# Differential attention scores: the low queries' pass over latent keys as two 64-row matmuls

## The chip, the cores and the metric

The kernel runs on one core of a Trainium2 chip. The metric is the time of one execution in device microseconds; the time before is 2394.58 us, the median of three runs.

## The reference, cut to what matters

Two layers of a hybrid backbone over 512 latent tokens and 256 context tokens, D = 1024, f32. In each layer one of three token mixers is differential attention with 4 heads. A head has two maps, each with its own 64 channels of query and key; both share a value of 128 channels. Latent queries read latent and context keys in one softmax, context queries (first layer only) read context keys alone.

```
def diff_attend(q, k, v, lam):
    s = jnp.einsum('bqhmd,bkhmd->bhmqk', q, k, preferred_element_type=jnp.float32) * (ATTN_HD ** -0.5)
    p = jax.nn.softmax(s, axis=-1)
    a = p[:, :, 0] - lam * p[:, :, 1]
    return jnp.einsum('bhqk,bkhe->bqhe', a.astype(v.dtype), v)
```

Around it stand the input projection of every branch, a pooling branch, a long convolution, the gates, the output projection and a SwiGLU network, all with f32 inputs.

## The kernel before, in words

**Number format.** TensorE multiplies fp32r operands. To keep f32 accuracy each operand is split into a high part, rounded to fp32r, and a low part, the rest. A product is then made of high by high, high by low and low by high; low by low is left out.

**Scores.** A head's map has 64 channels, half the 128 partitions, so one key tile of 128 partitions holds both parts of one map. `roped` (lines 992 to 1016) writes them: for map m, `k[m]` has the high keys in "own" partitions (0 to 63 for map 0, 64 to 127 for map 1) and the low keys in the other 64. For the queries there are two tiles for a map: `qz[m][0]` has the high queries in both halves, so that one matmul of 128 partitions gives high by high plus high by low; `qz[m][1]` has the low queries in the own half and zeros in the other (set once by GpSimd, line 1190 and after), so that a second matmul adds low by high. The `qz` tiles are the stationary operand (128 queries), the keys the moving one.

**One call.** `weights(h, q0, lat)` (line 1042) makes the attention weights of 128 queries. For latent queries it takes three PSUM tiles: `sl[0]` and `sl[1]` (512 latent keys, one for each map; "s" in the rows, line 1053) and `sct` (256 context keys of both maps; "sc", line 1054). It issues eight matmuls, four of 512 columns and four of 256. Then VectorE takes the maxima, first of `sct` and then of each `sl` (lines 1056 and 1059), ScalarE the exponentials (1066, 1070), and both the normalised difference `aw`. For context queries (layer 0 only) there is `sct` alone.

**Order.** Each head makes four calls for latent queries (blocks 0 to 3) and in layer 0 two for context queries, then turns and multiplies by values, in the order of `HEAD`. Between those steps `fill()` sets units of the input projection: line 285, the kernel's most frequent matmul, three passes for a weight tile. The program's text does not fix the order in which an engine gets its instructions: a planner orders them when the program is built. On each engine it takes the earliest instruction in program order that by its own reckoning can start; one whose PSUM tile has not been released, or whose input isn't there, is passed by later ones. PSUM tiles of tag "x" are four in layer 0 and five in layer 1, and the transposes, values and statistics use them too.

**Other half-array matmuls.** `mlp_steps` (line 608) multiplies f32 tiles by 64 x 64 weights, for two directions in opposite corners of the array; in layer 1's filters this stands amid line 285's stream. `first_norm` (line 403) uses 32 columns of the array for each of four products.

Of the kernel before, what the change touches and what calls it, by code (L numbers as in the profile page):

```python
# [18 lines left out]
L = 512  # L19
C = 256  # L20
T = L + C
# [123 lines left out]
def build(ctx: ExitStack, tc: tile.TileContext, io: dict, out: bass.AP, dbg=None):  # L145
    nc = tc.nc
    V, A, PE, SP, G = nc.vector, nc.scalar, nc.tensor, nc.sync, nc.gpsimd
# [34 lines left out]
    def PT(tag, n, shape, dt=F32):  # L182
        pool, size, cnt = tg[tag]
        assert int(np.prod(shape[1:])) * 4 <= size, (tag, n, shape)
        return pool.tile(shape, dt, tag=tag, name=nm(n), bufs=cnt)
# [10 lines left out]
    def TB(n, dt=F32, shape=None):  # L196
        return PT("b", n, shape or [P, 512], dt)
# [5 lines left out]
    def SM(n, w, bufs=4):  # L203
        return sm.tile([P, w], F32, tag=f"sm{w}x{bufs}", name=nm(n), bufs=bufs)
# [13 lines left out]
    def PX(n="x"):  # L218
        return ps["pool"].tile([P, 512], F32, tag="x", name=nm(n), bufs=4 + ps["layer"])
# [689 lines left out]
    def layer(l, a, hs, first, prepare):  # L909
# [83 lines left out]
        qkv = [{} for _ in range(HEADS)]  # L993
# [48 lines left out]
        def weights(h, q0, lat):  # L1042

            qs = slice(q0, q0 + P)
            sl = [PX("s"), PX("s")] if lat else None
            sct = PX("sc")
            scs = [sct[:, m * 256:m * 256 + 256] for m in range(2)]
            for m in range(2):
                y = qkv[h]["k"][m]
                for pi, x in enumerate(qz[m]):  # L1050
                    kw = dict(start=(pi == 0), stop=(pi == 1))
                    if lat:
                        PE.matmul(sl[m][:], x[:, qs], y[:, 0:L], **kw)  # L1053
                    PE.matmul(scs[m], x[:, qs], y[:, L:T], **kw)  # L1054
            mx = SM("mx", 8, bufs=6)
            V.tensor_reduce(out=mx[:, 0:2], in_=sct[:].rearrange("p (m k) -> p m k", m=2), axis=AX.X, op=ALU.max)
            if lat:
                for m in range(2):
                    V.tensor_reduce(out=mx[:, 2 + m:3 + m], in_=sl[m][:], axis=AX.X, op=ALU.max)
                V.tensor_tensor(out=mx[:, 0:2], in0=mx[:, 0:2], in1=mx[:, 2:4], op=ALU.max)  # L1060
            V.tensor_scalar(out=mx[:, 4:6], in0=mx[:, 0:2], scalar1=-0.125, scalar2=None, op0=ALU.mult)
            su = SM("su", 8, bufs=6)
            ec = TB("ec")
            el = []
            for m in range(2):
                A.activation(ec[:, m * 256:m * 256 + 256], scs[m], AF.Exp, scale=0.125, bias=mx[:, 4 + m:5 + m],
                             accum_out=su[:, m:m + 1])
                if lat:
                    e = TB("el")
                    A.activation(e[:], sl[m][:], AF.Exp, scale=0.125, bias=mx[:, 4 + m:5 + m],  # L1070
                                 accum_out=su[:, 2 + m:3 + m])
                    el.append(e)
            if lat:
                V.tensor_tensor(out=su[:, 0:2], in0=su[:, 0:2], in1=su[:, 2:4], op=ALU.add)
            V.reciprocal(su[:, 4:6], su[:, 0:2])
            V.tensor_tensor(out=su[:, 6:7], in0=su[:, 5:6], in1=nlam[:, l:l + 1], op=ALU.mult)
            aw = PT("aw", "aw", [P, T])
            for e0, e1, c0, nn in (([(el[0][:], el[1][:], 0, L)] if lat else [])
                                   + [(ec[:, 0:256], ec[:, 256:512], L, C)]):
                A.activation(aw[:, c0:c0 + nn], e0, AF.Copy, scale=su[:, 4:5])  # L1080
                V.scalar_tensor_tensor(out=aw[:, c0:c0 + nn], in0=e1, scalar=su[:, 6:7],
                                       in1=aw[:, c0:c0 + nn], op0=ALU.mult, op1=ALU.add)
            return aw
# [105 lines left out]
        qz = [[PT("qz", "qz", [P, W], F32R) for _ in range(2)] for _ in range(2)]  # L1189
# [30 lines left out]
        for h in range(HEADS):  # L1220
# [4 lines left out]
            m = {}  # L1225
            aws = {}
            awc = None
            for what in HEAD[l]:
                if what == "f":
                    fill()  # L1230
                elif what == "r":
                    rest()
                elif what in "0123":
                    aws[int(what)] = weights(h, int(what) * P, True)
                elif what == "c":
                    awc = [weights(h, L + i * P, False) for i in range(2)] if cx else None
                elif what in "AB":
                    i = 0 if what == "A" else 2
                    m[what] = turn([aws[i], aws[i + 1]], True)
                else:  # L1240
                    values(h, m["A" if what == "V" else "B"], 0 if what == "V" else 256, ot)
# [284 lines left out]
```

## Time and profile before

| What | Value |
| --- | --- |
| Time, median of 3 runs (lowest to highest) | 2394.58 us (2389.93 to 2403.16) |
| The profiled execution's own time | 2393.87 us |
| Its span, first to last instruction | 2392.1 us |
| Mean granted TensorE clock | 0.991 |
| TensorE matmul records, share of the span | 2325.6 us, 97% |
| VectorE, ScalarE | 1722.3 us (72%), 983.6 us (41%) |

Instructions are named by line, engine, operation and tiles: "out<-in", without buffer numbers. For a matmul the shape is given as partitions x columns of the weights, then partitions x columns of the moving operand. PE is TensorE's matmul, PEld its weight load, which runs beside. The ends of matmuls are modelled: matmuls are pipelined, and a recorded end lies after the start of the next one, so the stream is read from starts. In a timeline, neighbours of one kind are merged into one entry, with their count and the time from the first start to the last end.

### The profile page before, as it was taken

Reading aid. Unit: us, or ns where it says so; the run is one execution under the profiler, and the core shown is the slowest. Engines: PE = TensorE matmul, PEld = TensorE weight load, DVE = VectorE, ACT = ScalarE, POOL = GpSimd, SP = SyncE. Lnnn points to the kernel's source line nnn. Section 1 sums busy time; section 2 is a strip of 40 time slices with the busy share of each in tenths; the row PEclk is TensorE's granted clock in tenths of the full one; section 3 lists DMA queues with packets and bytes.
Section 4 is the critical chain, followed back from the end, with each engine's and each line's share of the span. In section 5 each row is a group of like instructions: output and inputs, shape, how many; then the busy total and the mean of one; then the engine's idle time right before and its main releaser. Section 6 shows DMA issues by size and latency. Waiting matters only on the chain. (4 is left out here: it accounts for less than half of the span.)

```text
span 2392.1 us, 33306 instructions
## 1 busy us (share of the span) xinstructions
PE 2325.6 (97%) x12834; PEld 1981.7 (83%) x12834; DVE 1722.3 (72%) x3135; ACT 983.6 (41%) x1657; POOL 2.7 (0%) x8
## 2 busy tenths in 40 slices
PE   6999899999999999999999999999999999999998
PEld 3888688888878878888888888888888789888888
DVE  5688877999888785666768726899888778333336
ACT  6433334367762352121133424433377635312223
POOL 0000000000000000000000000000000000000000
PEclk9999899999989999999999999999999999999999
DMA  7222132321137543444725525344311444332324
GB/s 265 71 96 81 44 103 71 124 95 67 45 133 253 185 156 130 130 146 158 232 88 170 167 98 162 125 165 162 119 56 46 168 152 154 113 97 95 96 92 150
DMA packets 117801, 302.47 MB, mean 126 GB/s; under 512 B 13445, under 2 KB 27397, under 8 KB 116618
## 3 DMA queue, kind: packets, MB, share of 16 engines
q1 hardware_dynamic: 117642, 300.34, 37.9%
q8 instruction: 101, 1.65, 0.3%
q14 instruction: 58, 0.48, 0.1%
HBM read 266.74 MB, written 33.55 MB: 126 GB/s over the span
## 5 line engine op out<-in xcount | busy, mean ns | idle before, releaser
L252 ACT CAST wh<-wr 128x1024 fp32r<-128x1024 f32 (+3 forms) x327 | 331.0, 1013 | 933.2 <-PE d L285 756.1
L285 PE MATMUL d<-ah,wh 128*128 128x512 f32 (+1 forms) x2320 | 707.4, 354 | 6.8 <-ACT si L1371 2.8
L285 PE MATMUL d<-al,wh 128*128 128x512 f32 (+1 forms) x2320 | 709.9, 354 | 0.1
L285 PE MATMUL d<-ah,wl 128*128 128x512 f32 (+1 forms) x2320 | 706.6, 353 | 2.1 <-DVE wl L253 2.0
L253 DVE TENSOR_TENSOR wl<-wr,wh 128x1024 fp32r<-128x1024 f32 (+3 forms) x327 | 383.5, 1173 | 163.4 <-ACT wh L252 153.5
L285 PEld LDWEIGHTS d<-ah,wh 128*128 128x128 f32 x2320 | 387.8, 188 | 71.7 <-ACT si L1371 3.2
L285 PEld LDWEIGHTS d<-ah,wl 128*128 128x128 f32 x2320 | 388.8, 188 | 64.1 <-DVE wl L253 3.0
L285 PEld LDWEIGHTS d<-al,wh 128*128 128x128 f32 x2320 | 389.0, 188 | 61.5 <-DVE al L350 0.8
L489 DVE SCALAR_TENSOR_TENSOR junk<-mr,cb 128x512 bf16<-128x512 f32 x256 | 176.4, 689 | 13.4 <-DMA mr<-in_w_mod_rows_dram 8.2
L285 PE MATMUL d<-hh,wh 128*128 128x512 f32 (+1 forms) x584 | 179.1, 341 | 3.4 <-DVE h L1406 3.4
L285 PE MATMUL d<-hh,wl 128*128 128x512 f32 (+1 forms) x584 | 178.9, 341 | 0.0
L285 PE MATMUL d<-hl,wh 128*128 128x512 f32 (+1 forms) x584 | 178.7, 341 | 0.0
L1380 DVE TENSOR_TENSOR si<-d,si 128x512 f32<-128x512 f32 (+2 forms) x48 | 36.9, 768 | 174.3 <-PE d L285 174.3
L285 PE MATMUL d<-xs,wh 128*128 128x512 f32 x576 | 145.0, 358 | 0.8 <-ACT mx L1183 0.6
L1406 DVE SCALAR_TENSOR_TENSOR h<-d,mod,h 128x512 f32<-128x512 f32 (+1 forms) x96 | 58.5, 615 | 83.3 <-PE d L285 83.0
L285 PEld LDWEIGHTS d<-hh,wh 128*128 128x128 f32 x584 | 102.4, 190 | 17.9 <-issue 3.8
L285 PEld LDWEIGHTS d<-hl,wh 128*128 128x128 f32 x584 | 102.2, 190 | 13.6
L285 PEld LDWEIGHTS d<-hh,wl 128*128 128x128 f32 x584 | 102.4, 190 | 13.1
L285 PEld LDWEIGHTS d<-xs,wh 128*128 128x128 f32 x576 | 94.7, 189 | 18.1 <-ACT mx L1183 0.9
L285 PE MATMUL d<-xs,wl 128*128 128x512 f32 (+1 forms) x288 | 87.7, 358 | 0.0
L795 DVE TENSOR_TENSOR Y<-Y,T 128x1024 f32<-128x1024 f32 (+1 forms) x80 | 84.7, 1059 | 0.2
L794 DVE TENSOR_TENSOR T<-U,K 128x1024 f32<-128x1024 f32 (+1 forms) x80 | 83.1, 1059 | 0.0
(294 smaller groups left out, 3207.8 us busy)
## 6 DMA issues: line engine op xcount, KB each, us to landing
wr<-in_w_in_dram SPq DMA_DIRECT2D x104, 512.0 KB, 3.4
wr<-in_w_ffn_in_dram SPq DMA_DIRECT2D x96, 512.0 KB, 3.3
mr<-in_w_mod_rows_dram SPq DMA_DIRECT2D x160, 256.0 KB, 3.6
wr<-in_w_out_dram SPq DMA_DIRECT2D x32, 512.0 KB, 3.3
ksp<-K SPq DMA_DIRECT2D x28, 384.0 KB, 2.8
K<-ksp SPq DMA_DIRECT2D x8, 1344.0 KB, 7.7
wr<-in_w_ffn_out_dram SPq DMA_DIRECT2D x24, 448.0 KB, 3.4
gsp<-gt SPq DMA_DIRECT2D x24, 384.0 KB, 2.5
```

What stands on the lines that cost most here:

```text
L252: A.copy(hi, src)
L253: V.tensor_tensor(out=lo, in0=src, in1=hi.bitcast(F32), op=ALU.subtract)
L285: PE.matmul(o, w[:, c0:c0 + P], x[k][xi][:, c:c + nn], start=(k == 0 and pi == 0), stop=(k == K - 1 and pi == 2))
L489: V.scalar_tensor_tensor(out=junk[:], in0=raw[hf], scalar=1.0, in1=cb[v][hf][:, 0:512], op0=ALU.mult, op1=ALU.mult, accum_out=pv[:, v, hf, ...
L794: V.tensor_tensor(out=t[:], in0=ub, in1=kb, op=ALU.mult)
L795: V.tensor_tensor(out=y[:], in0=y[:], in1=t[:], op=ALU.add)
L1380: V.tensor_tensor(out=sg[f][:, cs], in0=o, in1=sg[f][:, cs], op=ALU.mult)
L1406: V.scalar_tensor_tensor(out=hs[d][:, cs], in0=o, scalar=mods[l][:, 40 + d, s:s + 1], in1=hs[d][:, cs], op0=ALU.mult, op1=ALU.add)
```

## The change

In `weights`, the low queries' pass over latent keys no longer uses 128 partitions, of which 64 are zeros. It reads the own 64 partitions of `qz[m][1]` and of the keys alone: partitions 0 to 63 for map 0, 64 to 127 for map 1. Both of these matmuls are put behind the six others of the call, next to each other, and add into `sl[0]` and `sl[1]`. The passes over context keys and the zeroed tiles stay.

```diff
             sl = [PX("s"), PX("s")] if lat else None
             sct = PX("sc")
             scs = [sct[:, m * 256:m * 256 + 256] for m in range(2)]
+            ks = qkv[h]["k"]
             for m in range(2):
-                y = qkv[h]["k"][m]
-                for pi, x in enumerate(qz[m]):
-                    kw = dict(start=(pi == 0), stop=(pi == 1))
-                    if lat:
-                        PE.matmul(sl[m][:], x[:, qs], y[:, 0:L], **kw)
-                    PE.matmul(scs[m], x[:, qs], y[:, L:T], **kw)
+                if lat:
+                    PE.matmul(sl[m][:], qz[m][0][:, qs], ks[m][:, 0:L], start=True, stop=False)
+                for pi in range(2):
+                    PE.matmul(scs[m], qz[m][pi][:, qs], ks[m][:, L:T], start=(pi == 0), stop=(pi == 1))
+            if lat:
+                for m in range(2):
+                    own = slice(64 * m, 64 * m + 64)
+                    PE.matmul(sl[m][:], qz[m][1][own, qs], ks[m][own, 0:L], start=False, stop=True)
```

## Rows read from the trace of the kernel before

**Rows 1.** The page: span, matmul engine, chain that ended last by line.

```profile
span 2392.1 us, 33306 instructions
...
PE 2325.6 (97%) x12834; PEld 1981.7 (83%) x12834; DVE 1722.3 (72%) x3135; ACT 983.6 (41%) x1657; POOL 2.7 (0%) x8
...
PE d L285 22%; PE av L1109 1%; PE s L1053 1%; PE dx L285 0%; PE at L1094 0%; DVE wl L253 0%; PE sc L1054 0%; ACT wh L252 0%; PE sp L313 0%; PE d L1181 0%; ACT aw L1080 0%; ACT el L1070 0%; DVE pu L1156 0%; PE st L1125 0%; PE st L331 0%
```

**Rows 2.** Busy sums by stretch: stretch, its length, each engine's busy us (count), clock, DMA.

```profile
500.00:690.00 190.00, 182.33 (x1087) 156.71 (x1088) 168.12 (x422) 135.81 (x316) 0.00 (x0) 0.96 0.18 61
1730.00:1892.00 162.00, 157.88 (x911) 134.13 (x910) 136.48 (x314) 123.03 (x276) 0.00 (x0) 1.00 0.22 74
```

**Rows 3.** Groups by line and form, TensorE: count, busy us, mean ns, idle before.

```profile
L1053 PE MATMUL s<-k,qz 128*128 128x512 f32 x128 | 44.8, 418 | 3.2 <-DVE oq L302 1.4 <-ACT qz L1015 0.7 <-ACT el L1070 0.5
...
L1054 PE MATMUL sc<-k,qz 128*128 128x256 f32 x160 | 31.3, 289 | 1.0 <-DVE ot L296 0.9
```

**Rows 4.** Timeline of TensorE, first call: start us, us, what, count.

```profile
501.67 0.39 PE L1053 MATMUL s<-k,qz 128*128 128x512 f32 x1
501.90 0.27 PE L1054 MATMUL sc<-k,qz 128*128 128x256 f32 x1
502.01 0.40 PE L1053 MATMUL s<-k,qz 128*128 128x512 f32 x1
502.24 0.28 PE L1054 MATMUL sc<-k,qz 128*128 128x256 f32 x1
502.36 0.71 PE L1053 MATMUL s<-k,qz 128*128 128x512 f32 x2
```

**Rows 5.** Timeline of TensorE around the filter network's half-array block.

```profile
1222.56 0.51 PE L285 MATMUL d<-ah,wl 128*128 128x512 f32 x2
1223.01 1.07 PE L608 MATMUL ml<-fh,w 64*64 64x512 f32 x4
...
1224.47 0.51 PE L285 MATMUL d<-al,wh 128*128 128x512 f32 x2
```

**Rows 6.** The same block in narrow windows, entries apart.

```profile
1223.01 0.65 PE L608 MATMUL ml<-fh,w 64*64 64x512 f32 x2
...
1223.49 0.59 PE L608 MATMUL ml<-fh,w 64*64 64x512 f32 x2
...
1224.01 0.50 PE L285 MATMUL d<-ah,wh 128*128 128x512 f32 x1
```

**Rows 7.** Timeline of weight loads: line 403's f32 products, evenly spaced.

```profile
39.88 0.13 PEld L403 LDWEIGHTS mr<-wm,cact 128*32 128x32 f32 x4 [0.30 <-issue]
40.31 0.13 PEld L403 LDWEIGHTS mr<-wm,cact 128*32 128x32 f32 x4 [0.30 <-issue]
```

**Rows 8.** Timeline of weight loads around the block of rows 5.

```profile
1223.00 0.19 PEld L608 LDWEIGHTS ml<-fh,w 64*64 64x64 f32 x4 [0.25 <-issue]
1224.01 0.30 PEld L285 LDWEIGHTS d<-ah,wh 128*128 128x128 f32 x2 [0.81 <-issue]
```

**Rows 9.** Timeline of TensorE, rest of the second call.

```profile
508.10 0.74 PE L1054 MATMUL sc<-k,qz 128*128 128x256 f32 x4
508.69 0.63 PE L1053 MATMUL s<-k,qz 128*128 128x512 f32 x2
```

**Rows 10.** Timeline of TensorE between two maps of one call.

```profile
551.77 0.28 PE L285 MATMUL d<-ah,wh 128*128 128x256 f32 x1
...
659.36 0.28 PE L285 MATMUL d<-al,wh 128*128 128x256 f32 x1
```

**Rows 11.** Timeline of TensorE, start of the last head's first call.

```profile
1861.06 0.40 PE L1053 MATMUL s<-k,qz 128*128 128x512 f32 x1
```

**Rows 12.** Waits of TensorE, 500 to 690 us: total us, times, longest us.

```profile
PE av L1109 <- DVE atl L253: 1.7, 1, 1.7
```

**Rows 13.** Timeline of TensorE around the network's first half-array block.

```profile
1213.04 0.51 PE L285 MATMUL d<-ah,wl 128*128 128x512 f32 x2
...
1214.94 0.51 PE L285 MATMUL d<-al,wh 128*128 128x512 f32 x2
```

## The prediction

> **What bounds the kernel now.** I read the page first, for the engines and for the chain of work that ended last; the reader is to see TensorE busy 97% of the span, and its projection matmuls (line 285) the largest item of the chain, with waits far behind [rows 1]. Then the sums by stretch, over the two stretches in which scores are made (500 to 690 us for layer 0, 1730 to 1892 us for layer 1): TensorE's matmul records cover 182.33 of 190 us and 157.88 of 162 us [rows 2]. So there is 7.7 + 4.1 = 11.8 us in both together in which TensorE does nothing, and whatever is added to its stream there lengthens the kernel, apart from what falls into that. Third, the groups of TensorE's instructions: 128 score matmuls of 512 columns and 160 of 256 [rows 3]. 128 = 32 calls of weights() with latent queries (2 layers, 4 heads, 4 blocks) times two maps times two passes. Fourth the timeline of TensorE, for what one matmul takes of the stream: starts, since the recorded ends run past the next start. A 512-column one is followed 0.23 us later by the next instruction, a 256-column one after 0.11 to 0.12 us (501.67, 501.90, 502.01, 502.24) [rows 4].
>
> **What the change takes away and adds.** In each of the 32 calls two full 512-column matmuls go (2 x 0.23 = 0.46 us of stream) and two come that read 64 partitions of the queries and the keys, one the lower, one the upper, each into its own PSUM tile. The 160 score matmuls over context keys (sc) stay. No DMA, no ScalarE, VectorE or GpSimd instruction is added or moved in the program: the lower queries' zero halves are still needed by sc. The sc tile is complete two matmuls earlier, and VectorE's first maximum reads it; I give this nothing, since what waits on it is not TensorE's stream, which is filled from line 285 meanwhile.
>
> What a half matmul costs on this chip can be read from another part of this kernel: the filter network, line 608, has two 64-row, 64-column halves on opposite corners of the array in the middle of line 285's stream, at full clock [rows 5]. Three things are seen there.
>
> - The two halves start 0.01 us apart and end together: the two first pieces are one 0.65 us entry and the two second pieces one of 0.59 [rows 6]. (These are f32; each product is two pieces. A piece of f32 streams 0.43 us, by the even spacing of f32 weight loads [rows 7].) So two neighbours can share the time of one.
> - Going in: the last ordinary pair starts at 1222.56; pairs follow each other every 0.34 to 0.35 us, so its stream is over at 1222.91. The weight load of the halves starts only at 1223.00 [rows 5, 8]: 0.09 us. That load isn't hidden either, though ordinary loads start while the matmul before is still streaming: the first piece is recorded 0.65 long with its partner, the second 0.59, some 0.05 us for 64 columns of weights [rows 6].
> - Going out: the second pieces start at 1223.49 and stream 0.43, to 1223.92; the next full weight load starts at 1224.01, 0.09 us later [rows 6, 8], and the full matmul after it is recorded 0.50 us long against 0.39 to 0.40 of the same shape within the stream [rows 4, 6]: 0.11 us for 128 columns of weights in the open.
>
> As a check, from 1222.56 to 1224.47 is 1.91 us; less two ordinary pairs (0.70) and two pieces (0.86) leaves 0.35, and 0.09 + 0.05 + 0.01 + 0.09 + 0.11 = 0.35 [rows 5]. The score halves have 128 columns of weights, so both loads are in the open for 0.11 us: a switch costs 0.09 + 0.11 = 0.20, in and out **0.40 us a block**. The trace has no half of 64 rows with all 128 columns, nor one in fp32r; the bounds are zero (between full matmuls of different lines and tiles nothing lies open, as the even starts show [rows 4], and a half that keeps every column might be no switch at all) and 0.40 plus a half that streams at f32's 2 x 0.43 us in place of 0.23. I take 0.40 and 0.23: the rows at 1222 us are the nearest.
>
> One rule of the Trainium skill bears on this. The page "TensorEngine Tiling (Array Packing)", section "Key Properties", has it that changing the tiling mode, as against the tile, drains the engine. By that a switch is paid here as in the rows (the sum below stands); if 64 rows of 128 columns did not count as another mode, the sum would be the third rival's.
>
> **Are the two halves neighbours?** The program order says so, but the order on TensorE is made by the planner, which lets an instruction pass earlier ones that can't start. Before, a call's eight matmuls ran in program order, 0.23 and 0.12 us apart, only where PSUM tiles and queries were all ready, as at 501.67 [rows 4]. Otherwise it is cut: the second call's first map had both passes at 502.36, its four sc at 508.10 and the second map's two passes at 508.69, as its PSUM tiles were released [rows 4, 9]. In the changed order, the low half of map 0 waits for nothing but its own high pass; so in a cut call it is put right behind that, as its full predecessor was, and the half of map 1 stands alone microseconds later. At 551.77 and 659.36 line 285 enters between the maps, though buffers are free, because the queries of map 1 aren't there yet [rows 10]; those are cut too. Going through both stretches in this way, 4 of the 32 calls have everything ready (the first of layer 0's head 0 and of layer 1's heads 1, 2 and 3; the last is at 1861.06 [rows 11]) and 28 are cut.
>
> **The sum.** A neighbouring pair: 0.40 + 0.23 + 0.01 = 0.64 for 0.46, +0.18 us; four of them +0.7. A half by itself: 0.40 + 0.23 = 0.63 for 0.23, +0.40; 28 calls with two each, 56 x 0.40 = +22.4. Together +23.1 us of stream. Some of it falls where TensorE had nothing to do: the longest wait there is 1.7 us, on VectorE [rows 12]; of the 11.8 us I take a third, 4 us. So +19 us. The profiled execution has 2393.87 us (span 2392.1 and 1.8 around it), 0.7 below the median of 2394.58, which is nothing; 2393.9 + 19 = **2413 us**. Next on VectorE, each map's maximum starts up to 0.8 us later in a cut call; VectorE is busy 168.12 of 190 us there [rows 2], so that delay can be made up.
>
> **Rivals.** With S for the two switches of a block, the change is 56 S + 4 (S - 0.22) = 60 S - 0.9 us when 28 calls are cut.
>
> 1. The planner keeps every pair together (it puts the low halves last, once both maps are there). 32 x 0.18 = +5.8, 2399.7 us. For it: they are adjacent in the program. Against it: in the cut calls of before, passes of one map ran as soon as they could.
> 2. The halves stream at the f32 pace: 56 x (0.40 + 0.63) + 4 x (0.18 + 0.63) = 61 us, 2455 us. For it only that the halves in the trace are f32; against it, that fp32r runs at 0.23 everywhere else.
> 3. The other side, not slower: a half that uses all 128 columns is no switch, its load is hidden like any other, S is 0. Cut calls cost nothing, neighbours save 0.22: -0.9 us, 2393 us; with all 32 neighbours -7.0 us, 2387 us. It decides from S below 0.015 us, and stays within the measurement's 0.5% (12 us) up to S = 0.21. For it: no such half is in the trace. Against it: in the filter network even a 33-row product goes in and out with the same gaps (1213.04 to 1214.94, 1.90 us) [rows 13]. The page "TensorE: Matmul & The Clock Gate" of the Trainium skill, section "Measured speedup vs the span model", prices a pack of tiles as one matmul and about 4 ns for each further tile, with nothing for going in and out; by that, with all neighbours, it is this rival's 2387. The trace agrees with the few ns and not with the rest.
> 4. The halves run as before, one behind the other at 0.23 us, or the price falls wholly into waits and a changed order: 2394 us, with 8 us to either side for the order.
>
> **How the numbers follow.** Forecast 0.60, rival 1 0.14, rival 2 0.05, rival 3 0.13, rival 4 0.08. A measurement of this kernel can tell 0.5%, 12 us, from no change. Slower by more than that: nearly all of the forecast (0.57) and rival 2: 0.62. Faster: the tails of rivals 3 and 4, 0.05. Within: 0.33. The forecast alone has 2405 (all of the idle time takes some) to 2420 (none does, all calls cut: 64 x 0.40 = 25.6). The range goes down to 2392 to take in rivals 1, 4's middle and the upper part of 3, and up to 2424; rival 2 and the rest of 3 are left out.
>
> **What would show it.** In the changed kernel's timeline a score matmul of 64 rows should stand alone in most calls, with the next full weight load starting some 0.3 us after it, 0.09 us after its stream, and the full matmul behind recorded 0.50 long; four calls should show two halves 0.01 us apart. The two score stretches should be longer by some 19 us in all, with the count of line 285's matmuls unchanged. Wrong it is if loads behind a half start with it (rival 3), if pairs are everywhere (rival 1), or if halves are spaced 0.8 us (rival 2).

## The result, and the profile after

The changed kernel takes 2414.93 us (median of 6, 2411.61 to 2421.95) against 2396.06 us for the kernel before in the same comparison: +18.9 us, ratio 1.0082, 95% interval 1.0059 to 1.0105 (14 to 25 us). It is slower; 2413 us were forecast, +19 us. The profiled execution has 2411.61 us.

First the page after: span, the engines' busy shares, and the granted clock in 40 slices.

```profile
span 2409.8 us, 33306 instructions
...
PE 2345.1 (97%) x12834; PEld 1980.4 (82%) x12834; DVE 1722.3 (71%) x3135; ACT 983.2 (41%) x1657; POOL 2.7 (0%) x8
...
PEclk9999899999999999999999999999999999999999
```

Against [rows 1] the counts are the same to the instruction, VectorE and ScalarE are as busy as they were, and only TensorE's records grew, by 19.5 us. TensorE's listed waits from 500 to 720 us add up to 7.5 us before and after alike; the stream itself is longer.

The timeline of TensorE after, in the first and second call, answers to [rows 4, 9]: start us, us, what, count.

```profile
501.31 0.40 PE L1053 MATMUL sc<-k,qz 128*128 128x256 f32 x2
501.64 0.49 PE L1057 MATMUL s<-k,qz 64*128 64x512 f32 x2
502.07 0.50 PE L1051 MATMUL s<-k,qz 128*128 128x512 f32 x1
502.50 0.50 PE L1057 MATMUL s<-k,qz 64*128 64x512 f32 x1
502.93 0.62 PE L285 MATMUL d<-ah,wh 128*128 128x512 f32 x2
...
508.24 0.74 PE L1053 MATMUL sc<-k,qz 128*128 128x256 f32 x4
508.82 0.39 PE L1051 MATMUL s<-k,qz 128*128 128x512 f32 x1
509.14 0.50 PE L1057 MATMUL s<-k,qz 64*128 64x512 f32 x1
509.57 0.62 PE L285 MATMUL d<-ah,wl 128*128 128x512 f32 x2
```

And the weight loads beside the second of these:

```profile
508.70 0.19 PEld L1051 LDWEIGHTS s<-k,qz 128*128 128x128 f32 x1
509.14 0.18 PEld L1057 LDWEIGHTS s<-k,qz 64*128 64x128 f32 x1 [0.25 <-issue]
509.57 0.30 PEld L285 LDWEIGHTS d<-ah,wl 128*128 128x128 f32 x2 [0.24 <-issue]
```

At 508.70 an ordinary load starts 0.12 us ahead of its matmul, under the stream of the one before. The load of the half does not: the full matmul of 508.82 has streamed out at 509.05, and the load starts at 509.14. After the half it is the same again: the full load starts at 509.57 with its matmul, whose entry is 0.11 us longer (0.62) than that of an ordinary pair (0.51 in [rows 5]). From 509.05 to 509.57 + 0.11 is 0.63 us for a matmul that streams 0.23. The two neighbours at 501.64 start in one entry of 0.49 and cost the same once: 501.54 to 502.07 + 0.11, 0.64 us for what took 0.46.

In all the timeline shows 62 blocks: 60 halves by themselves and 2 with two halves. Read in this way, their median is 0.625 us. That makes 60 x (0.625 - 0.231) + 2 x (0.63 - 0.462) = 24.0 us more stream, 0.231 us being the stream of one full matmul.

### The profile page after: what moved, and what is told of

It reads as the page before. It is cut to its first block, busy times and chain, and to the rows that moved or that the text cites. A ratio compares the mean times of both kernels' runs of the same rounds, so it can differ in the third digit from the quotient of the medians.

```text
span 2409.8 us, 33306 instructions
## 1 busy us (share of the span) xinstructions
PE 2345.1 (97%) x12834; PEld 1980.4 (82%) x12834; DVE 1722.3 (71%) x3135; ACT 983.2 (41%) x1657; POOL 2.7 (0%) x8
## 4 chain that ended last, share of the span: by engine, by line
PE 89%; DVE 6%; ACT 2%; issue 2%; DMA 1%; SPq 0%; DVEq 0%; ACTq 0%
PE d L285 74%; DVE wl L253 1%; PE av L1112 1%; PE dx L285 1%; PE s L1057 1%; PE fg L672 1%; PE sc L1053 1%; PE at L1097 1%; PE yo L880 1%; ACT wh L252 1%; PE s L1051 1%; PE zo L863 1%; PE gre L701 1%; DVE T L810 0%; PE mr L403 0%
```

## Experiments

Theory: the time goes to switching the array from whole to halves and back, 0.40 us a block, and most halves are blocks of their own because the planner parts the pairs. (A block is a run of half matmuls with no other matmul between them.) Rivals: the new order of the passes costs it (PSUM tiles held longer, VectorE served later); each half matmul pays, whether it has a neighbour or not; any matmul over fewer than 128 partitions pays.

**Full matmuls in the new order.** The planner puts TensorE's instructions in exactly the order of the changed kernel.

```diff
-                    own = slice(64 * m, 64 * m + 64)
-                    PE.matmul(sl[m][:], qz[m][1][own, qs], ks[m][own, 0:L], start=False, stop=True)
+                    PE.matmul(sl[m][:], qz[m][1][:, qs], ks[m][:, 0:L], start=False, stop=True)
```

> The low pass over latent keys stays at the end of the call, as in the changed kernel, but reads all 128 partitions again. Theory (the price is the switch of the array between whole and halves, 0.40 us in and out of each block): no block is left, so the time is that of the kernel before, 2396 us within 5. Rival (the price is the new order: passes at the end of a call, PSUM tiles held longer, VectorE and ScalarE served later): the time stays near 2415 us.

Measured 2395.47 us, ratio 0.9993 (0.9983 to 1.0003) to before. Timeline of TensorE, the instructions that stand at 502.07 to 502.93 after:

```profile
502.83 0.47 PE L1051 MATMUL s<-k,qz 128*128 128x512 f32 x1
503.14 0.39 PE L1056 MATMUL s<-k,qz 128*128 128x512 f32 x1
503.36 0.51 PE L285 MATMUL d<-ah,wh 128*128 128x512 f32 x2
```

The low pass is followed after 0.22 us, not 0.43, and the pair behind it is 0.51 long, not 0.62. The order is worth nothing; the whole +18.9 us belongs to the halves. The rival of the order is out.

**Fewer partitions without halves.** Map 0's low pass reads partitions 0 to 95, map 1's all 128.

```diff
-                    own = slice(64 * m, 64 * m + 64)
+                    own = slice(0, 96 + 32 * m)
```

> The low pass at the end of the call, map 0 over partitions 0 to 95 (the 32 beyond its own hold zeros), map 1 over all 128. Theory (the price is that of switching the array into halves and back, not of fewer partitions): no switch, 2396 us within 5, the weight load behind starts while the matmul streams. Rival (any matmul with fewer than 128 partitions makes the array drain): 32 blocks, 0.39 us each, 2406 to 2408 us.

Measured 2395.45 us, ratio 0.9991 (0.9981 to 1.0000). Timelines of matmuls, then of loads:

```profile
502.95 0.47 PE L1051 MATMUL s<-k,qz 128*128 128x512 f32 x1
503.26 0.39 PE L1057 MATMUL s<-k,qz 96*128 96x512 f32 x1
```

```profile
503.03 0.19 PEld L1057 LDWEIGHTS s<-k,qz 96*128 96x128 f32 x1
503.26 0.19 PEld L285 LDWEIGHTS d<-ah,wh 128*128 128x128 f32 x1
```

The load of 96 rows starts 0.23 us before its matmul, and the full load behind starts with that matmul, under its stream. So not every matmul over fewer than 128 partitions pays: 96 rows run as the whole array does, 64 rows as halves.

**Half the dose.** Only map 1's low pass is a half; each call has one.

```diff
+                    if lat and (m, pi) != (1, 1):
+                        PE.matmul(sl[m][:], qz[m][pi][:, qs], ks[m][:, 0:L], start=(pi == 0),
+                                  stop=(m == 0 and pi == 1))
...
+                own = slice(64, 128)
+                PE.matmul(sl[1][:], qz[1][1][own, qs], ks[1][own, 0:L], start=False, stop=True)
```

> Map 0's low pass is a full matmul in its old place; only map 1's is a half, at the end of the call. 32 halves, each alone. Theory: 32 x 0.394 = 12.6 us of stream more than before, less some 2 us that fall into idle time: 2406 to 2409 us. If neighbours' sharing were what is missing and a lone half cost nothing, 2396 us.

Measured 2405.95 us against 2396.68 before, ratio 1.0032 (1.0020 to 1.0045), 7.7 us with an interval of 5 to 11: two fifths of the change's price, and within the interval half of it, for half of its blocks, at the low edge of what was expected. The 32 blocks have the same median, 0.625 us, so the stream is 12.6 us longer; that the missing 3 to 5 us fell into time that was lost before is likely, but was not traced.

**The pairs kept together.** Both halves are queued behind the second map's high pass and go first there.

```diff
-                    PE.matmul(sl[m][:], qz[m][0][:, qs], ks[m][:, 0:L], start=True, stop=False)
+                    hi = PE.matmul(sl[m][:], qz[m][0][:, qs], ks[m][:, 0:L], start=True, stop=False)
...
-                for m in range(2):
-                    own = slice(64 * m, 64 * m + 64)
-                    PE.matmul(sl[m][:], qz[m][1][own, qs], ks[m][own, 0:L], start=False, stop=True)
+                with tc.issue_after(hi.ins), tc.high_priority(offset=3000):
+                    for m in range(2):
+                        own = slice(64 * m, 64 * m + 64)
+                        PE.matmul(sl[m][:], qz[m][1][own, qs], ks[m][own, 0:L], start=False, stop=True)
```

> The two halves of a call may stand only behind the second map's high pass, and come first there, so that in 30 of 32 calls they are neighbours on TensorE; 4 stand alone. Theory (a price for each block of halves, and neighbours share one block and one stream): 30 x (0.63 - 0.46) + 4 x (0.625 - 0.23) = 5.1 + 1.6 = 6.7 us over the kernel before, some 2402 us, a ratio of 1.003 to before. Rival A (a price for each half matmul, wherever it stands): still 64 halves, near 2415 us. Rival B (the order): the second map's maximum waits longer still, 2415 us or more.

Measured 2424.88 us, ratio 1.0102 (1.0083 to 1.0122): a miss, +24 us by the ratio where 6.7 was expected. On the time alone rival B held, and rival A (near 2415 us) could hold with some of B on top. The timeline in this kernel:

```profile
501.31 0.40 PE L1051 MATMUL s<-k,qz 128*128 128x512 f32 x1
501.64 0.50 PE L1058 MATMUL s<-k,qz 64*128 64x512 f32 x2
502.07 0.51 PE L1053 MATMUL sc<-k,qz 128*128 128x256 f32 x2
...
678.09 0.73 PE L1053 MATMUL sc<-k,qz 128*128 128x256 f32 x4 [3.39 <-ACT el L1074]
```

The pairs stand as meant, 30 of them, and each block is again about 0.63 us, so two halves do share one price. But at 678 us TensorE stands still for 3.39 us until the exponentials release a PSUM tile; nothing of the kind is in the changed kernel.

**The pairs kept, as full matmuls.** The same order on TensorE to the instruction, with whole-array low passes.

```diff
-                        own = slice(64 * m, 64 * m + 64)
-                        PE.matmul(sl[m][:], qz[m][1][own, qs], ks[m][own, 0:L], start=False, stop=True)
+                        PE.matmul(sl[m][:], qz[m][1][:, qs], ks[m][:, 0:L], start=False, stop=True)
```

> The kernel with the pairs kept, with the same order on TensorE, but both low passes read all 128 partitions. Theory (the pairs cost what the switches cost, 5 to 7 us; the rest of that kernel's 24 us is that the low passes wait for the second map, and PSUM tiles and TensorE with them): some 18 us over the kernel before, 2414 us, 5 to 8 us under the pairs kept. Rival (neighbours do not help, each half matmul costs 0.3 to 0.4 us): 2397 us, 24 us under the pairs kept.

Measured 2413.63 us, ratio 1.0067 (1.0054 to 1.0080). TensorE's waits, 495 to 720 us: total us, times, longest us.

```profile
PE sc L1053 <- ACT el L1073: 5.8, 2, 3.4
PE at L1097 <- ACT el L1073: 3.5, 2, 1.9
```

The changed kernel's longest wait in the same stretch, for comparison:

```profile
PE av L1112 <- DVE atl L253: 1.9, 1, 1.9
```

So holding the low passes back until the second map is there costs some 16 us by itself, with full matmuls. Not all of it need be waits: the granted clock was 0.985 to 0.987 in the five executions of this kernel and 0.987 to 0.992 in those of the kernel before beside them, and what that takes of the 16 us was not separated. The two ratios differ by 0.0035, 8.4 us (3 to 14 from the two intervals, and the runs are of two comparisons): that is what 30 pairs and 4 lone halves cost, 6.7 us expected. Had each of the 64 halves paid 0.394 us for itself, the difference would have been some 25.

**Four half matmuls in a block.** As with the pairs kept, each half in two matmuls of 256 columns.

```diff
+                    for c in (0, 256):
+                        for m in range(2):
+                            own = slice(64 * m, 64 * m + 64)
+                            PE.matmul(sl[m][:, c:c + 256], qz[m][1][own, qs], ks[m][own, c:c + 256],
+                                      start=False, stop=(c == 256))
```

> As with the pairs kept, but each half is made as two matmuls of 256 columns, so that a block holds four half matmuls in place of two and there are twice as many half matmuls in all, with the same columns. Theory (the price is paid at the two switches of a block, not inside it): within 3 us of the kernel with the pairs kept, some 2402 us; weight loads that a half must make twice could add up to 0.1 us a block, 3 us. Rival (each half matmul pays): 64 more of them, 0.2 to 0.4 us each, 13 to 25 us more.

Measured 2421.52 us, ratio 1.0102 (1.0081 to 1.0124): the same as with two halves in a block, as the theory has it, though both are 20 us or more above the absolute time that was expected, most of it for the reason just shown. Timeline of its first block:

```profile
501.20 0.51 PE L1059 MATMUL s<-k,qz 64*128 64x256 f32 x4
501.64 0.51 PE L1053 MATMUL sc<-k,qz 128*128 128x256 f32 x2
```

From the halves' start to the next full start is 0.44 us with four, 0.43 with two (501.64 to 502.07 above). Inside a block two more half matmuls, with the same columns in all, cost 0.01 us. The price lies at its two ends.

## Why the prediction was right, point by point

- **What bounds the kernel**: right. TensorE's stream was lengthened and the kernel with it.
- **The price of a switch**, 0.40 us a block: right, 0.394, taken from a block of another shape (f32, 64 columns, opposite corners). The gap before the half's load (0.09), the load in the open, the gap behind and the full load in the open (0.11) are all there. The rival of a free switch is refuted by the loads after, that of a half at f32's pace by blocks of 0.63 us.
- **Neighbours or not**: right in kind, off in number. 28 cut calls and 4 pairs were forecast; 60 halves stand alone and there are 2 pairs, of which one is made of halves of two successive calls (556.51). In layer 1 the first calls of heads 1, 2 and 3, read as whole, are cut too: the planner puts the first map's half ahead of the second map's high pass, as in the last head:

```profile
1874.57 0.39 PE L1053 MATMUL sc<-k,qz 128*128 128x256 f32 x2
1874.90 0.49 PE L1057 MATMUL s<-k,qz 64*128 64x512 f32 x1
1875.32 0.50 PE L1051 MATMUL s<-k,qz 128*128 128x512 f32 x1
```

  By program order that half comes after; I had read "everything ready" from matmuls that followed each other without a gap [rows 4, 11], which says when they ran and not that the later ones could have started sooner. (The planner's reckoning is in no trace; this is read from the order that it made.) It made the stream 24.0 us longer in place of 23.1.
- **What idle time takes**: 4 us was a guess, a third of the idle time; that it came out near is luck. The profiled executions differ by 17.7 us, 6.3 less than the stream, and this has two causes. The first score of layer 0 starts at 500.88 before and 500.53 after, the first of layer 1 at 1732.07 before and 1737.36 after: layer 0 and what follows it gives +5.6 us where its 28 lone halves and 2 pairs make 11.4; from layer 1's scores to the end it is +12.4, and 32 lone halves make 12.6. Neither part can be read as it stands, since the granted clock fell in different places in the two executions. In the first part the kernel before had two stretches at the lower clock that the profiled execution after did not have. Sums by stretch, the last but two numbers being the granted clock, before:

```profile
845.00:865.00 20.00, 16.85 (x125) 16.28 (x124) 16.73 (x42) 9.48 (x13) 0.00 (x0) 0.91 0.63 210
1465.00:1485.00 20.00, 16.00 (x99) 15.20 (x98) 18.31 (x31) 11.66 (x18) 0.00 (x0) 0.83 0.44 142
```

  and after:

```profile
853.00:873.00 20.00, 17.32 (x139) 16.45 (x138) 17.62 (x44) 10.84 (x15) 0.00 (x0) 1.00 0.67 220
1472.00:1492.00 20.00, 15.44 (x109) 14.17 (x108) 19.73 (x33) 11.62 (x19) 0.00 (x0) 1.00 0.51 159
```

  In these places the lead of the kernel before (how much sooner it starts the same weight cast) shrinks by some 4 us together: 8.53 to 6.34 us and 7.30 to 5.42. In layer 1 it is the other way round. The kernel after has a stretch at the lower clock from 1894 us on, after three waits of TensorE (0.72, 0.52 and 1.18 us); the kernel before, with 0.92, 0.52 and 1.38 us in the same places, has none. After, then before:

```profile
1894.71 0.77 PE L1051 MATMUL s<-k,qz 128*128 128x512 f32 x1 [1.18 <-DVE oq L302]
1901.21 0.64 PE L285 MATMUL d<-xs,wh 128*128 128x512 f32 x2
1894.00:1901.20 7.20, 6.14 (x14) 4.05 (x15) 6.07 (x15) 4.52 (x6) 0.00 (x0) 0.53 0.52 163
```

```profile
1880.02 0.69 PE L1053 MATMUL s<-k,qz 128*128 128x512 f32 x2 [1.38 <-DVE oq L302]
1883.77 0.63 PE L285 MATMUL d<-xs,wh 128*128 128x512 f32 x2
1880.00:1883.80 3.80, 3.23 (x15) 2.38 (x16) 3.77 (x11) 3.40 (x5) 0.00 (x0) 1.00 0.31 88
```

  The same work takes 6.50 us after and 3.75 before; less 0.40 for the block of one half in it, the clock cost some 2.35 us. Without it layer 1's part is some +10 us, 2.5 less than its halves make. Layer 0's scores end with the kernel before 8.53 us ahead, from 0.35 behind at their start: +8.9, again 2.5 less, at a granted clock of 0.96 from 500 to 690 us before [rows 2] and after. So some 5 us of the added stream did not lengthen the kernel (an estimate from one execution of each kernel), against the 4 forecast, and the clock took some 2 us more in the kernel before than in the one after. The stream was forecast 0.9 us too short and the idle time's share some 1 us too small; these cancel, which is luck and helped the number.

  What took up these 5 us is not settled: the listed waits hardly shrank. Neither were the places of the low clock explained: the mean granted clock is 0.991 in both profiled executions, and in the kernel with half the dose both stretches of the first part are low again (0.91 and 0.83).
- **Rival 1** (the planner keeps every pair) did not occur. Forced, it cost +24 us, not +5.8: the rival's price for the pairs is borne out (8.4 us, 3 to 14), but the rival had no term for holding the passes back.
- **The rules of pages**: the rule of the Trainium skill, "TensorEngine Tiling (Array Packing)", "Key Properties", that a change of mode drains the array, agrees with this trace, at 0.09 us from the end of the stream to the next load, and 0.11 more for that load, which isn't hidden. The span model of the Trainium skill, "TensorE: Matmul & The Clock Gate", "Measured speedup vs the span model", agrees inside a block (two halves in one entry, four of half the columns in 0.01 us more than two) and has no term for its two ends, which here are nearly twice the matmul.

## What to carry to other kernels

Two half-array matmuls side by side do take the time of one, but the block costs 0.40 us at its ends against the 0.23 us that a pair of 512 columns gives back; from these numbers (an estimate, not run) a block needs at least two such pairs before it gains, amid full matmuls. Where a planner orders the instructions, program order does not keep neighbours together; and forcing them together can cost more than the switch, by what waits for the held tile. No version here beats the kernel before: the two in the new order that have no halves equal it.

## What the runs showed that was not expected

- 96 partitions run without a switch (ratio 0.9991), 64 with: leaving the zeros of the stationary operand out by halves costs more, at this size, than multiplying them.
- Holding 64 passes of 0.23 us behind their sister map, with full matmuls and no other change, costs 0.67% of the kernel; in its profiled execution TensorE stands still for 3.4 us at one place where the kernel before does not.
